# Bonus sums in a hybrid RWKV block: two 128x512 products become four float32 strips, and a transfer spreads the result

## The chip, the cores and the metric

The kernel runs on one core of one Trainium2 chip. The metric is the device time of one execution in microseconds; before the change it is 992.68 us, the median of three runs (991.85 to 993.29). A further execution was profiled. It took 991.71 us; its span, from the first to the last instruction, is 989.6 us, so 2.1 us lie around the span. In this text a place like "at 293.8" is a time in that span in microseconds.

## What is computed

One layer of a streaming encoder on 528 positions (16 learned meta tokens and 512 frames) of width 2048. One input projection with 8320 columns feeds two groups: an RWKV-7 time mixing with 16 heads of 64, and a short gated convolution with 1024 channels. Cut to what matters here:

```
P  = rmsnorm(h) @ w_in                     # 2048 x 8320
r, k, v, g_r = token-shifted columns of P  # 1024 wide each, 16 heads x 64
kk = (k * k_k) per head, divided by its norm
k  = k * (1 + (a - 1) * k_a)
y  = delta-rule recurrence of r, decay, k, v, kk, kk * a   # per head
yn = group norm of y per head
bonus = sum over the head of (r * k * r_k), times v
y_a = (yn + bonus) * silu(g_r)
y_b = B * conv3(C * h) * silu(g_c)
out = rmsnorm(h_res + concat(y_a, y_b) @ w_out)
```

The change concerns the line of the bonus. For every head and position there is one number, the sum of 64 products; it is multiplied with the 64 channels of v.

## The kernel before, in words

**Precision.** The large projections run as products of float32r parts. Every operand is split into a high part (a cast on ScalarE) and a low part (a subtraction on VectorE), and three of the four products are added up in PSUM. A tile of the input projection is 128 columns wide; its 2048 rows of contraction are done as four quarters of 512, and each quarter of weights has its own cast (L151) and its own subtraction (L152), `w<-wr` in the trace. TensorE takes the quarters one after another (L353 for the tiles with a token shift, L368 for the tiles B and gc).

**Order.** TensorE follows an order written out by hand. The tiles of the projection are a stream (`mains`); between its matmuls stands the rest of TensorE's work. `fill(ns)` takes so many estimated nanoseconds of stream matmuls. `later(ns, fn)` puts a transfer or an operation into the program when the stream has advanced by ns from now, and `until("v", i)` runs the stream until v of pair i exists. VectorE, ScalarE, GpSimd and the queue of SyncE (SP) are ordered by a scheduler from the order of the code and from priorities; on each of them an instruction that waits holds up all that stand behind it.

**Pairs.** The 16 heads are worked on as 8 pairs; a pair is a tile of 128 rows, 64 for each head. `prepare(i)` computes for pair i the decays, the operands of the recurrence (`ar`, `bk`), the Gram matrices `gt` (L755, L766), and the inverses of 16x16 blocks (`d`, `nd`, `y`, `prod`, `tt`: a chain of some thirty small VectorE operations, L855 to L888). The chain starts with `tt<-d,nd` (L862). Two pairs then go through `invert`.

**Norms of the keys.** The squared norms are sums over the 64 rows of a head. `key_norms` (L786) computes them as four matmuls in plain float32: 128 rows by 32 columns of a 0/1 matrix (`cs`), each with 144 positions and each in a column strip of its own of the array. The result lies in the first PSUM bank of the next stream tile, which is borrowed for this; `n2` (L781, `n` in the trace) takes it to SBUF, and two small stores (`sn<-n`) and a load (`nd<-sn`) bring it into the layout of the chain.

**Bonus.** After r, k and r_k have been multiplied in place into `r` (L735), `r` is split (L665 on ScalarE, L666 on VectorE). Two float32r matmuls with a 128x128 matrix `ones` (L820, L821) sum over the 64 rows of each head and at once spread the sum over 64 rows, into the bank `zb`. ScalarE copies `zb` back to `r` (L822), VectorE multiplies by v (L919), and the product is stored (`rbd<-r`, L920) until the output stage loads it.

**Convolution group.** A tile h is scaled in two halves by VectorE (`hh`, L404, with a small `ex`, L403, between them). GpSimd multiplies (`u`, L485), ScalarE takes the first tap (`cv`, L487), and VectorE adds the other two (L490). In the program these stand among the casts and subtractions of the weights. The second group of such tiles is called C1, h1, B1, gc1 here; it comes right behind pair 3.

Of the kernel before, what the change touches and what calls it, by code (L numbers as in the profile page):

```python
# [9 lines left out]
F32 = mybir.dt.float32  # L10
F32R = mybir.dt.float32r
I32 = mybir.dt.int32
AF = mybir.ActivationFunctionType
ALU = mybir.AluOpType
# [4 lines left out]
P = 128  # L19
DM = 2048  # L20
KT = DM // P
SEQ = 512
META = 16
L = SEQ + META
CH = 64
NCH = SEQ // CH + 1
LP = NCH * CH
# [5 lines left out]
C_ID, C_GM, C_BM, C_ON = 0, 128, 384, 512  # L33
# [11 lines left out]
    tr=3200, lev=3000, cp=4200, out=1500, begin=19500, p=2900, u=2900, s=4200, mid=1000, last=3700, mix=2600,  # L45
# [44 lines left out]
def hymba_kernel(ctx: ExitStack, tc: tile.TileContext, xt, xtok, front, w_in, w_out, pv, lup, cst, msk, gf, out):  # L90
    nc = tc.nc
    ctx.enter_context(tc.manual_schedule(engines={mybir.EngineType.PE}))
    cp = ctx.enter_context(tc.tile_pool(name="cp", bufs=1))
    dp = ctx.enter_context(tc.tile_pool(name="dp", bufs=2, space=DRAM))
# [3 lines left out]
    cs = cp.tile([P, C_N], F32, name="cs")  # L98
# [6 lines left out]
    rbd = [dp.tile([P, SEQ], F32, tag=f"rbd{j}", name=f"rbd{j}", bufs=1) for j in range(NPAIR)]  # L105
# [63 lines left out]
    xp = ph1.enter_context(tc.tile_pool(name="xp", bufs=1))  # L169
# [3 lines left out]
    rst = xp.tile([P, 4], F32, name="rst")  # L173
    rsx = cq.tile([P, 2 * META], F32, name="rsx")
    la = cq.tile([P, 2, L], F32R, name="la")
    ones = xp.tile([P, P], F32R, name="ones")
    omm = xp.tile([P, 33], F32, name="omm")
    hv = xp.tile([P, 6, 8], F32, name="hv")
    hl = cp.tile([P, 2, 8], F32, name="hl")
# [3 lines left out]
    pi = ph1.enter_context(tc.tile_pool(name="pi", bufs=1, space=PSUM))  # L183
# [5 lines left out]
    def tr(name, dt=F32):  # L189
        return cq.tile([P, LP], dt, tag="tr", name=name, bufs=5)  # L190
# [122 lines left out]
    with tc.issue_after(head):  # L313
        nc.vector.tensor_scalar(
            out=omm, in0=pvt[:, V_MU : V_MU + 33], scalar1=-1.0, scalar2=1.0, op0=ALU.mult, op1=ALU.add
        )
        for d, off in (
# [4 lines left out]
                out=d, in0=pvt[:, off : off + 8], scalar1=0.5, scalar2=None, op0=ALU.mult  # L322
            )
        nc.vector.tensor_scalar(
            out=hv[:, 4], in0=pvt[:, V_KA : V_KA + 8], scalar1=-0.5, scalar2=1.0, op0=ALU.mult, op1=ALU.add
        )

    nc.scalar.copy(ones, cs[:, C_BM : C_BM + P])
    FULL = ((0, 272), (272, L))
    TAIL = ((14, 272), (272, L))  # L330
    REAL = ((META, L),)
# [264 lines left out]
    def later(ns, fn):  # L596
        pending.append((clock[0] + ns, fn))
        pending.sort(key=lambda e: e[0])
# [60 lines left out]
        nc.vector.tensor_tensor(out=lo, in0=raw, in1=hi.bitcast(F32), op=ALU.subtract)  # L659
        return hi, lo  # L660

    def split(t, name, n):
        hi = tr(f"{name}_h", F32R)[:, 0:n]
        lo = tr(f"{name}_l", F32R)[:, 0:n]
        nc.scalar.copy(hi, t)  # L665
        nc.vector.tensor_tensor(out=lo, in0=t, in1=hi.bitcast(F32), op=ALU.subtract)  # L666
        return hi, lo

    heads = [(h, slice(64 * h, 64 * h + 64), slice(64 - 64 * h, 128 - 64 * h)) for h in range(2)]

    place = [(i % 2) * 4 + i // 2 for i in range(NPAIR)]
# [11 lines left out]
    def behind(dst, src):  # L683
        with tc.issue_after(state["dma"]):
            nc.sync.dma_start(dst, src)
# [8 lines left out]
    def prepare(i):  # L694
# [22 lines left out]
            out=bk[:, :, 0], in0=c3(k), scalar=hv[:, 2, i : i + 1], in1=c3(te), op0=ALU.mult, op1=ALU.mult  # L717
# [3 lines left out]
            out=ta, in0=ta, scalar1=hv[:, 3, i : i + 1], scalar2=hv[:, 4, i : i + 1], op0=ALU.mult, op1=ALU.add  # L721
        )
        nc.vector.scalar_tensor_tensor(
            out=ar[:, :, 0], in0=c3(k), scalar=col(V_KK, i), in1=e1[:, :, 0:CH], op0=ALU.mult, op1=ALU.mult
# [6 lines left out]
        r = got["r", i]  # L731
        nc.vector.tensor_tensor(
            out=ar[:, 1:NCH, 1], in0=c3(r), in1=e1[:, 1:NCH, 1 : CH + 1], op=ALU.mult
        )
        nc.vector.scalar_tensor_tensor(  # L735
            out=r, in0=r, scalar=hv[:, 5, i : i + 1], in1=ta[:, CH:LP], op0=ALU.mult, op1=ALU.mult
        )

        sq = tr(f"sq{i}")
        nc.scalar.activation(sq, k, AF.Square, scale=col(V_KK, i))  # L740
        rh, rl = split(r, f"rk{i}", SEQ)
        fill(FW["gram_b" if p else "gram"] + FW["meta"].get(i, 0))

        late = state["step"] > 48
# [16 lines left out]

        def gram_meta():
            z = early or next_banks()
            norms = key_norms(z[0][:, 96 : 96 + NS]) if late else None
            for h, hs, ho in heads:
                nc.tensor.matmul(  # L766
                    z[h][:, 0:META],
                    bk[hs, 0, h : h + 2, :].rearrange("p a s -> p (a s)"),
                    ar[hs, 0, 0, 0:META],
                    start=True, stop=True,  # L770
                )
            norms = norms if late else key_norms(z[0][:, 96 : 96 + NS])
            if p and "levels" in state:
                state["out"] = state.pop("levels").pop(0)(second_level(z))
            with ahead():
                for h in range(2):
                    nc.vector.tensor_tensor(
                        out=gt[:, h, 0, 0:META], in0=z[h][:, 0:META], in1=gmask[:, h, 0:META], op=ALU.mult
                    )
            with ahead():  # L780
                nc.scalar.copy(n2, norms)  # L781
            if "out" in state:
                state.pop("out")()
            state["banks"] = z

        def key_norms(z):  # L786
            for j in range(4):
                nc.tensor.matmul(
                    z[32 * j : 32 * j + 32], cs[:, C_BM + 48 : C_BM + 80], sq[:, j * NS : (j + 1) * NS],
                    start=True, stop=True, tile_position=(0, 32 * j),  # L790
                )
            return z
# [11 lines left out]

        NS = LP // 4
        n2 = tr(f"n2{i}")[:, 0:NS]
        if late:
            gram_meta()
        za = [pz.tile([P, 4, P], F32, tag="tz", name=f"g{i}_1_{h}") for h in range(2)]
# [6 lines left out]
        masked(zc, 5, 9)  # L816
        fill(FW["gram2"] - FW["meta"].get(i, 0))

        zb = pi.tile([P, SEQ], F32, tag="ser", name=f"zb{i}")
        nc.tensor.matmul(zb, ones[:, 0:P], rh, start=True, stop=False)  # L820
        nc.tensor.matmul(zb, ones[:, 0:P], rl, start=False, stop=True)  # L821
        nc.scalar.copy(r, zb)  # L822
        fill(FW["misc"])


# [4 lines left out]
        sg = dp.tile([SCR], F32, tag="sg", name=f"sg{i}")  # L830
        sn = dp.tile([2 * LP], F32, tag="sn", name=f"sn{i}")
        sx = scr_x[i % 2]

        def rows(t, h):
            return bass.AP(tensor=t.tensor, offset=t.offset + h * NCH * 4 * BLK, ap=[[CH, CH], [4 * BLK, NCH], [1, CH]])
# [3 lines left out]

        for h in range(2):  # L840
            behind(sn[h * LP : (h + 1) * LP].rearrange("(j s) -> j s", s=NS), n2[16 - 16 * h : P : 32])
        for h in range(2):
            behind(rows(sg, h), gt[64 * h : 64 * h + 64, h, :, 0:CH])
        NB = 8 * NCH
# [23 lines left out]
        for m in (2, 4, 8):  # L868
            for b in range(16 // (2 * m)):
# [4 lines left out]
                    out=pq,  # L874
                    in0=sub(d, o, o + m, [[16, m], [0, m], [1, m]]),
                    in1=sub(y, o + m, o + m, [[0, m], [1, m], [16, m]]),
                    op=ALU.mult,
                )
                nc.vector.tensor_reduce(
                    out=tq.rearrange("p (i j) -> p i j", i=m), in_=pq, op=ALU.add, axis=AX.X  # L880
                )
                nc.vector.tensor_tensor(
                    out=pq,
                    in0=sub(y, o, o, [[16, m], [0, m], [1, m]]),
                    in1=bass.AP(tensor=tq.tensor, offset=tq.offset, ap=[list(tq.ap[0]), [0, m], [1, m], [m, m]]),
                    op=ALU.mult,
# [19 lines left out]
        for h, hs, ho in heads:  # L906
            for b in range(2):
                for a in range(2):
                    later(9000 + 900 * (4 * h + 2 * b + a), lambda h=h, b=b, a=a: nc.sync.dma_start(
                        bass.AP(  # L910
                            tensor=bd.tensor,
                            offset=bd.offset + (h ^ a) * (NCH - 1) * CH * NPAIR * P + place[i] * P + 64 * h + 32 * b,
# [3 lines left out]
                    ))  # L916
        until("v", i)
        v = got["v", i]
        nc.vector.tensor_tensor(out=r, in0=r, in1=v[:, CH:LP], op=ALU.mult)  # L919
        later(12500, lambda: nc.sync.dma_start(rbd[i], r))  # L920
        fill(FW["v"])

        vs = cq.tile([P, NCH, CH], F32, tag="vs", name=f"vs{i}")
# [1 line left out]
        for b in range(4):  # L925
            for t in range(2):
                later(14000 + 1000 * (2 * b + t), lambda b=b, t=t: nc.sync.dma_start(
                    bass.AP(
                        tensor=vd.tensor,
# [736 lines left out]
```

## Time and profile before

| | before |
|---|---|
| median of three runs | 992.68 us |
| the profiled execution | 991.71 us |
| its span | 989.6 us |
| TensorE busy | 980.0 us, 99% |
| VectorE busy | 706.8 us, 71% |
| ScalarE busy | 390.6 us, 39% |
| GpSimd busy | 127.8 us, 13% |
| TensorE's share of the chain that ended last | 95% |

The matmuls overlap in the trace, so the duration of one is longer than the time it takes from its successor. What a matmul costs TensorE is read from the start of it to the start of the next. In rows of the timeline the columns are: start, duration of the merged instructions, engine, line, operation, output and inputs by their names, size of the tile of the array, moving operand, count, and in brackets the idle time before and what ended it.

### The profile page before, as it was taken

To read this page: it belongs to the slowest core of one execution; us is meant where nothing else is said; L and a number is where in the kernel's file an instruction comes from. 1 tells how busy PE (TensorE), PEld (TensorE's weight loads), DVE (VectorE), ACT (ScalarE), POOL (GpSimd) and SP (SyncE) were. 2 spreads that over 40 slices of the span, in tenths; PEclk is the share of its full clock that TensorE was granted. 3 is DMA by queue.
4 is the path that set the end of the run, shared out by engine and by line. 5 is a ranking of instruction groups with operands and counts; after the bars stand their busy time and mean duration, and the time that the engine had idled before them with its cause. 6 is when DMAs were issued, how large, how long until landed. Compare 5 with 4: busy or idle time off the path is not lost.

```text
span 989.6 us, 23395 instructions
## 1 busy us (share of the span) xinstructions
PE 980.0 (99%) x9511; PEld 907.5 (92%) x9511; DVE 706.8 (71%) x1413; ACT 390.6 (39%) x731; POOL 127.8 (13%) x242
## 2 busy tenths in 40 slices
PE   9999999999999999999999999999999999999996
PEld 9999999999998999998999998889889898788885
DVE  7777966578675779653778654365756697998896
ACT  7553432343322434322434323232323335446454
POOL 0110302112010111010111010011211102001001
PEclk9999999999999999999999999999999999999999
DMA  9526586246684375853275856999886697697554
GB/s 325 156 91 152 143 206 164 82 130 145 153 199 150 92 187 123 209 153 115 89 176 125 202 143 192 275 253 258 229 267 167 181 300 182 180 320 189 150 128 171
DMA packets 205532, 176.91 MB, mean 179 GB/s; under 512 B 138544, under 2 KB 168048, under 8 KB 205040
## 3 DMA queue, kind: packets, MB, share of 16 engines
q1 hardware_dynamic: 202832, 166.50, 60.2%
q0 software_dynamic: 2304, 8.39, 5.0%
q8 instruction: 75, 1.23, 0.5%
q10 hardware_dynamic: 288, 0.52, 0.1%
q14 instruction: 33, 0.27, 0.1%
HBM read 139.02 MB, written 36.35 MB: 177 GB/s over the span
## 4 chain that ended last, share of the span: by engine, by line
PE 95%; DVE 3%; ACT 1%; issue 1%; DMA 0%; DVEq 0%; POOL 0%; ACTq 0%
PE ps_v L353 9%; PE ps_h L353 9%; PE ps_C L353 9%; PE ps_g L353 9%; PE ps_B L368 9%; PE ps_gc L368 9%; PE ps_k L353 8%; PE ps_r L353 8%; PE M L1383 5%; PE P L1383 4%; PE Q L1383 2%; PE g L755 2%; PE ps_k L368 1%; PE ps_r L368 1%; PE ps_lora L368 1%; PE zy L1141 1%
## 5 line engine op out<-in xcount | busy, mean ns | idle before, releaser
L151 ACT CAST w<-wr 128x512 fp32r<-128x512 f32 x252 | 153.7, 619 | 285.1 <-PE ps_C L353 44.8
L152 DVE TENSOR_TENSOR w<-wr,w 128x512 fp32r<-128x512 f32 x252 | 174.8, 705 | 116.4 <-ACT w L151 115.5
L353 PE MATMUL ps_v<-xh,w 128*128 128x256 f32 (+2 forms) x512 | 84.0, 285 | 0.0
L368 PE MATMUL ps_B<-xh,w 128*128 128x512 f32 x256 | 83.4, 394 | 0.0
L353 PE MATMUL ps_h<-xh,w 128*128 128x256 f32 (+2 forms) x512 | 81.7, 281 | 0.0
L353 PE MATMUL ps_g<-xh,w 128*128 128x256 f32 (+2 forms) x512 | 81.4, 281 | 0.0
L368 PE MATMUL ps_gc<-xh,w 128*128 128x512 f32 x256 | 81.2, 392 | 0.0
L353 PE MATMUL ps_C<-xh,w 128*128 128x256 f32 (+2 forms) x512 | 80.8, 280 | 0.0
L353 PEld LDWEIGHTS ps_v<-xh,w 128*128 128x128 f32 x512 | 73.9, 188 | 0.3
L353 PE MATMUL ps_k<-xh,w 128*128 128x256 f32 (+1 forms) x448 | 73.4, 285 | 0.0
L353 PEld LDWEIGHTS ps_g<-xh,w 128*128 128x128 f32 x512 | 72.0, 189 | 0.6 <-issue 0.2
L353 PE MATMUL ps_r<-xh,w 128*128 128x256 f32 (+1 forms) x448 | 72.5, 280 | 0.0
L353 PEld LDWEIGHTS ps_h<-xh,w 128*128 128x128 f32 x512 | 72.1, 189 | 0.3
L353 PEld LDWEIGHTS ps_C<-xh,w 128*128 128x128 f32 x512 | 71.8, 189 | 0.2
L353 PEld LDWEIGHTS ps_k<-xh,w 128*128 128x128 f32 x448 | 64.7, 188 | 0.4
L353 PEld LDWEIGHTS ps_r<-xh,w 128*128 128x128 f32 x448 | 63.5, 189 | 0.4 <-issue 0.2
L353 PE MATMUL ps_h<-xl,w 128*128 128x256 f32 x256 | 57.3, 281 | 0.0
L368 PEld LDWEIGHTS ps_gc<-xh,w 128*128 128x128 f32 x256 | 47.8, 188 | 10.0
L368 PEld LDWEIGHTS ps_B<-xh,w 128*128 128x128 f32 x256 | 47.8, 188 | 9.7
L353 PE MATMUL ps_C<-xl,w 128*128 128x256 f32 x256 | 56.2, 280 | 0.0
L353 PE MATMUL ps_v<-xl,w 128*128 128x256 f32 x256 | 55.8, 278 | 0.0
L353 PE MATMUL ps_g<-xl,w 128*128 128x256 f32 x256 | 55.4, 278 | 0.0
(382 smaller groups left out, 2144.5 us busy)
## 6 DMA issues: line engine op xcount, KB each, us to landing
wr<-in_w_in_dram SPq DMA_DIRECT2D x126, 512.0 KB
ct<-opd SPq DMA_DIRECT2D x72, 192.0 KB
wo<-in_w_out_dram SPq DMA_DIRECT2D x24, 512.0 KB
x<-in_w_out_dram POOLq DMA_DIRECT2D x16, 512.0 KB, 5.6
opd<-ar SPq DMA_DIRECT2D x8, 576.0 KB
opd<-gt SPq DMA_DIRECT2D x16, 288.0 KB
bd<-bt SPq DMA_DIRECT2D x64, 64.0 KB
bw<-bd SPq DMA_DIRECT2D x16, 256.0 KB
```

Of the source, the lines that this page charges most:

```text
L151: nc.scalar.copy(hi, rq)
L152: low[q] = eng.tensor_tensor(out=lo, in0=rq, in1=hi.bitcast(F32), op=ALU.subtract).ins
L353: nc.tensor.matmul(ps[r][:, 0 : b - a], ww[:, k * P : (k + 1) * P], xx[:, kt, a:b], start=(kt == 0 and n == 0), stop=(kt == KT - 1 and n = ...
L368: nc.tensor.matmul(ps[r], ww[:, w], xx[:, kt, a:b], start=(kt == 0 and n == 0), stop=(kt == KT - 1 and n == 2))
L755: nc.tensor.matmul(z[h][:, c - c0], bk[hs, c, h : h + 2, :].rearrange("p a s -> p (a s)"), ar[hs, c].rearrange("p a s -> p (a s)"), start= ...
L1141: nc.tensor.matmul(zy[e][hs if e else ho, k], t[hs, o : o + CH], x, start=(n == 0), stop=(n == 2))
L1383: nc.tensor.matmul(bank[s], left(prod, jj, m, s), w, start=(jj == 0 and n == 0), stop=(jj == 7 and n == 2))
```

## The change

The split of `r`, the matrix `ones`, the bank `zb` and its copy go. The four float32 strips of `key_norms` become a function of their input (`head_sums`), which is called twice in a row: on the squared keys with 144 positions each, into the first borrowed bank, as before; and on `r` itself with 128 positions each, into the second borrowed bank. A copy of 128x128 on ScalarE (`nb`) stands behind that of the norms. Two stores of 4x128 numbers (`sb<-nb`) are put in 1000 ns later, a load of 128x512 that repeats each of the two rows over 64 partitions (`r<-sb`) 4500 ns later. The product with v is no longer done where v exists but 10500 ns after that place, and its store 15500 ns after it instead of 12500.

```
@@ prepare(i)
-        rh, rl = split(r, f"rk{i}", SEQ)
...
         def gram_meta():
             z = early or next_banks()
-            norms = key_norms(z[0][:, 96 : 96 + NS]) if late else None
+            if late:
+                norms, bonus = sums_of(z)
...
-            norms = norms if late else key_norms(z[0][:, 96 : 96 + NS])
+            if not late:
+                norms, bonus = sums_of(z)
...
             with ahead():
                 nc.scalar.copy(n2, norms)
+                nc.scalar.copy(nb, bonus)
...
-        def key_norms(z):
+        def sums_of(z):
+            return head_sums(z[0][:, 96 : 96 + NS], sq, NS), head_sums(z[1][:, 96 : 96 + P], r, P)
+
+        def head_sums(z, x, n):
             for j in range(4):
                 nc.tensor.matmul(
-                    z[32 * j : 32 * j + 32], cs[:, C_BM + 48 : C_BM + 80], sq[:, j * NS : (j + 1) * NS],
+                    z[32 * j : 32 * j + 32], cs[:, C_BM + 48 : C_BM + 80], x[:, j * n : (j + 1) * n],
                     start=True, stop=True, tile_position=(0, 32 * j),
                 )
             return z
...
-        zb = pi.tile([P, SEQ], F32, tag="ser", name=f"zb{i}")
-        nc.tensor.matmul(zb, ones[:, 0:P], rh, start=True, stop=False)
-        nc.tensor.matmul(zb, ones[:, 0:P], rl, start=False, stop=True)
-        nc.scalar.copy(r, zb)
...
+        for h in range(2):
+            later(1000, lambda h=h: nc.sync.dma_start(
+                sb[h * SEQ : (h + 1) * SEQ].rearrange("(j s) -> j s", s=P), nb[16 * h : P : 32]
+            ))
+        later(4500, lambda: nc.sync.dma_start(r, bass.AP(tensor=sb.tensor, offset=sb.offset, ap=[[SEQ, 2], [0, CH], [1, SEQ]])))
...
-        nc.vector.tensor_tensor(out=r, in0=r, in1=v[:, CH:LP], op=ALU.mult)
-        later(12500, lambda: nc.sync.dma_start(rbd[i], r))
+        later(10500, lambda: nc.vector.tensor_tensor(out=r, in0=r, in1=v[:, CH:LP], op=ALU.mult))
+        later(15500, lambda: nc.sync.dma_start(rbd[i], r))
```

The first place where the order of instructions changes is TensorE in each pair: the two products with `ones` stand between stream matmuls, at pair 1 at the end of a tile g. Before, TensorE at pair 1:

```order
L353 MATMUL ps_g_1_1663<-xl,w_1495 128x256 x4
L353 MATMUL ps_g_1_1663<-xh,w_1495 128x260 x4
L353 MATMUL ps_g_1_1663<-xh,w_1495 128x258 x3
L820 MATMUL zb_1808<-rk_h,ones 128x512
L821 MATMUL zb_1808<-rk_l,ones 128x512
L353 MATMUL ps_g_1_1663<-xh,w_1495 128x258
L353 MATMUL ps_C_0_1742<-xl,w_1555 128x256
```

After the change that place holds stream matmuls alone. The strips stand about 25 rows earlier, behind those of the norms; of the changed kernel, TensorE at pair 1 (`g_5` and the first two `ps_C` rows are the Gram matrices, `sq` the squared keys, `r` the products to be summed):

```order
L745 MATMUL g_5_0_1721<-ar_1355,bk_1356 128x128
L745 MATMUL g_5_1_1722<-ar_1355,bk_1356 128x128
L757 MATMUL ps_C_0_1739<-ar_1355,bk_1356 128x16
L757 MATMUL ps_C_1_1740<-ar_1355,bk_1356 128x16
L784 MATMUL ps_C_0_1739<-sq_1539,cs 32x144 x4
L784 MATMUL ps_C_1_1740<-r_1309,cs 32x128 x4
L351 MATMUL ps_g_1_1659<-xh,w_1370 128x258 x3
```

Two matmuls are gone from one place, and four strips stand at another, right behind strips of the same shape.

The second place is VectorE at the start of pair 3's chain, in the last tile before h1. `ex<-ps_C` can only run when TensorE has finished tile C1. Before:

```order
L861 COPY y_3669<-nd_3666 72x16
L152 TENSOR_TENSOR w_3752<-wr_3747,w_3752 128x512
L862 TENSOR_TENSOR tt_3674<-d_3665,nd_3666 72x8
L863 TENSOR_TENSOR y_3669<-tt_3674,nd_3666 72x8
L873 TENSOR_TENSOR prod_3673<-d_3665,y_3669 72x8
L948 STREAM_TRANSPOSE xn_4065<-xT_3080 128x512
L879 TENSOR_REDUCE tt_3674<-prod_3673 72x4
L882 TENSOR_TENSOR prod_3673<-y_3669,tt_3674 72x8
L152 TENSOR_TENSOR w_3781<-wr_3779,w_3781 128x512
L888 TENSOR_REDUCE y_3669<-prod_3673 72x2x2
L403 TENSOR_TENSOR ex<-ps_C_1_3513,rst 128x4
```

After, on the same engine and at the same place:

```order
L860 COPY y_3672<-nd_3669 72x16
L152 TENSOR_TENSOR w_3756<-wr_3751,w_3756 128x512
L401 TENSOR_TENSOR ex<-ps_C_1_3514,rst 128x4
L861 TENSOR_TENSOR tt_3677<-d_3668,nd_3669 72x8
L918 TENSOR_TENSOR r_3151<-r_3151,v_3325 128x512
L862 TENSOR_TENSOR y_3672<-tt_3677,nd_3669 72x8
L872 TENSOR_TENSOR prod_3676<-d_3668,y_3672 72x8
L947 STREAM_TRANSPOSE xn_4071<-xT_3081 128x512
L878 TENSOR_REDUCE tt_3677<-prod_3676 72x4
L881 TENSOR_TENSOR prod_3676<-y_3672,tt_3677 72x8
L887 TENSOR_REDUCE y_3672<-prod_3676 72x2x2
L152 TENSOR_TENSOR w_3786<-wr_3784,w_3786 128x512
```

The chain's first seven operations, the transpose `xn` among them, and one subtraction of weights stand behind the `ex` of tile C1 now, not ahead of it, and the product with v stands among them; before, that product stood some twenty rows earlier.

The third place is VectorE at the end of the same chain. Before:

```order
L873 TENSOR_TENSOR prod_3673<-d_3665,y_3669 72x512
L879 TENSOR_REDUCE tt_3674<-prod_3673 72x64
L882 TENSOR_TENSOR prod_3673<-y_3669,tt_3674 72x512
L888 TENSOR_REDUCE y_3669<-prod_3673 72x8x8
L404 TENSOR_TENSOR hh_4007<-ps_h_0_3884,rs 128x256
L403 TENSOR_TENSOR ex<-ps_h_1_3885,rst 128x4
L404 TENSOR_TENSOR hh_4007<-ps_h_1_3885,rs 128x256
L490 SCALAR_TENSOR_TENSOR cv_4014<-u_3870,pvt,cv_4014 128x512 x2
```

After:

```order
L872 TENSOR_TENSOR prod_3676<-d_3668,y_3672 72x512
L878 TENSOR_REDUCE tt_3677<-prod_3676 72x64
L402 TENSOR_TENSOR hh_4013<-ps_h_0_3889,rs 128x256
L881 TENSOR_TENSOR prod_3676<-y_3672,tt_3677 72x512
L401 TENSOR_TENSOR ex<-ps_h_1_3890,rst 128x4
L402 TENSOR_TENSOR hh_4013<-ps_h_1_3890,rs 128x256
L887 TENSOR_REDUCE y_3672<-prod_3676 72x8x8
L488 SCALAR_TENSOR_TENSOR cv_4020<-u_3875,pvt,cv_4020 128x512 x2
```

The two halves of `hh` have moved ahead of the chain's last reduction.

More of the change, by code (lines that the diff above doesn't have):

```diff
@@ L175, in hymba_kernel @@
     la = cq.tile([P, 2, L], F32R, name="la")
-    ones = xp.tile([P, P], F32R, name="ones")
     omm = xp.tile([P, 33], F32, name="omm")
@@ L326, in hymba_kernel @@
         )
-    nc.scalar.copy(ones, cs[:, C_BM : C_BM + P])
     FULL = ((0, 272), (272, L))
@@ L660, in lora_up @@
         return hi, lo
[L662 to L667, printed above, removed]
     heads = [(h, slice(64 * h, 64 * h + 64), slice(64 - 64 * h, 128 - 64 * h)) for h in range(2)]
@@ L806, in prepare @@
         n2 = tr(f"n2{i}")[:, 0:NS]
+        nb = tr(f"nb{i}")[:, 0:P]
         if late:
@@ L832, in prepare @@
         sx = scr_x[i % 2]
+        sb = dp.tile([2 * SEQ], F32, tag="sb", name=f"sb{i}")
         def rows(t, h):
```

## The prediction, as it was put on record

> **What bounds the kernel now.** I read the page's busy times and chain first, then the list of waits on TensorE.
>
> ```profile
> span 989.6 us, 23395 instructions
> PE 980.0 (99%) x9511; PEld 907.5 (92%) x9511; DVE 706.8 (71%) x1413; ACT 390.6 (39%) x731; POOL 127.8 (13%) x242
> PE 95%; DVE 3%; ACT 1%; issue 1%; DMA 0%; DVEq 0%; POOL 0%; ACTq 0%
> ```
>
> ```profile
> PE pwarm L202 <- DVE cold L199: 1.0, 1, 1.0
> PE M L1383 <- DVE o L1352: 0.3, 1, 0.3
> ```
>
> TensorE is busy for 99% of the span and carries 95% of the chain. In the whole run it waits twice, 1.3 us together, and neither wait lies where the change works. So a microsecond saved on another engine is worth nothing, one on TensorE is worth itself, and the change can lose only by making TensorE wait where it does not wait now. I therefore count TensorE's matmuls first and then look for the place where the other engines come close to it.
>
> **The change on TensorE.** The two products with `ones`, at pair 4, and the four strips of the key norms, at pair 1:
>
> ```profile
> 399.05 0.39 PE L820 MATMUL zb<-rk_h,ones 128*128 128x512 f32 x1
> 399.28 0.39 PE L821 MATMUL zb<-rk_l,ones 128*128 128x512 f32 x1
> 399.50 0.28 PE L353 MATMUL ps_g<-xl,w 128*128 128x256 f32 x1
> ...
> 122.62 0.45 PE L788 MATMUL ps_C<-sq,cs 128*32 128x144 f32 x8
> 122.76 0.31 PE L788 MATMUL ps_C<-sq,cs 128*32 128x144 f32 x4
> 123.00 0.39 PE L353 MATMUL ps_g<-xh,w 128*128 128x258 f32 x1
> ```
>
> Start to start, the two products cost 399.50 - 399.05 = 0.45 us. The strips of the norms cost 123.00 - 122.62 = 0.38 us: the first stretch lasts 0.14 us (122.62 to 122.76), and the last one 0.24 us with the way back to the stream in it. Eight new strips in the same form, right behind, should repeat the inner part alone: two stretches of 0.14 us, shortened from 144 to 128 positions, 2 x 0.14 x 128/144 = 0.25 us. The trace has no second set behind a first one, so I bound this: below by 0.12 us (one stretch, if the sets overlap), above by 0.38 us (a set of its own with all its ends). I take 0.25, because both new and old strips write disjoint strips of the array in the same way. The gain is 0.45 - 0.25 = 0.20 us in each of 8 pairs, 1.6 us in all; by the bounds 0.07 to 0.33 a pair, 0.6 to 2.6 us.
>
> [...]
>
> **What goes from and comes to the other engines.**
>
> ```profile
> L665 ACT CAST rk_h<-r x8: 620/621/624, 76.6 to 529.7; 128x512 fp32r<-128x512 f32 x8
> ...
> L822 ACT COPY r<-zb x8: 579/587/589, 89.0 to 546.8; 128x512 f32<-128x512 f32 x8
> ...
> L781 ACT COPY n<-ps_C x2: 278/278/279, 124.2 to 258.1; 128x144 f32<-128x144 f32 x2
> ...
> L666 DVE TENSOR_TENSOR rk_l<-r,rk_h x8: 677/690/694, 78.4 to 530.4; 128x512 fp32r<-128x512 f32 x8
> ...
> L919 DVE TENSOR_TENSOR r<-r,v x8: 685/692/694, 89.7 to 547.4; 128x512 f32<-128x512 f32 x8
> ...
> L685 SPq DMA_DIRECT2D sn<-n x16: 494/538/607, 85.8 to 544.9; - x16
> ```
>
> Per pair ScalarE loses a cast (0.62) and a copy (0.59) and gains a copy of about 0.28; VectorE loses a subtraction (0.69) and keeps its product (0.69); SyncE's queue gains two small stores of about 0.54 and the issue of one load. ScalarE is busy 39% of the span and VectorE 71%, so by themselves these are worth nothing. The second borrowed bank is free again when the new copy has read it, at pair 1 some 0.6 us behind 124.2, and the tile that owns it begins only here:
>
> ```profile
> 129.52 0.28 PE L353 MATMUL ps_C<-xl,w 128*128 128x256 f32 x1
> ```
>
> The loads of weights behind the new issues start a microsecond or two later. What hides that is in the page's row of the casts:
>
> ```profile
> L151 ACT CAST w<-wr 128x512 fp32r<-128x512 f32 x252 | 153.7, 619 | 285.1 <-PE ps_C L353 44.8
> ```
>
> The idle time ahead of them is ended by TensorE, which frees their buffers, and not by a landing: the loads are early. Were that cover gone, each microsecond would be one of TensorE's.
>
> **The place where it bites: tile B1, behind pair 3.** The order shows pair 3's chain entering VectorE behind `ex` of tile C1 instead of ahead of it. VectorE of before:
>
> ```profile
> 273.19 0.15 DVE L862 TENSOR_TENSOR tt<-d,nd 72x8 f32<-72x8 f32 x1
> ...
> 274.44 0.16 DVE L882 TENSOR_TENSOR prod<-y,tt 72x8 f32<-72x8 f32 x1
> 275.32 0.69 DVE L152 TENSOR_TENSOR w<-wr,w 128x512 fp32r<-128x512 f32 x1 [0.71 <-ACT w L151]
> 275.93 0.15 DVE L888 TENSOR_REDUCE y<-prod 72x4 f32<-72x8 f32 x1
> 277.42 0.16 DVE L403 TENSOR_TENSOR ex<-ps_C,rst 128x4 f32<-128x4 f32 x1 [1.34 <-PE ps_C L353]
> ...
> 287.20 0.68 DVE L888 TENSOR_REDUCE y<-prod 72x64 f32<-72x512 f32 x1
> 287.80 0.41 DVE L404 TENSOR_TENSOR hh<-ps_h,rs 128x256 f32<-128x256 f32 x1
> 288.65 0.16 DVE L403 TENSOR_TENSOR ex<-ps_h,rst 128x4 f32<-128x4 f32 x1 [0.44 <-PE ps_h L353]
> 288.73 0.41 DVE L404 TENSOR_TENSOR hh<-ps_h,rs 128x256 f32<-128x256 f32 x1
> ...
> 292.85 2.49 DVE L152 TENSOR_TENSOR w<-wr,w 128x512 fp32r<-128x512 f32 x4
> ```
>
> Today VectorE does the chain's start in time that it would otherwise spend waiting (1.34 us) for TensorE to end C1. After that `ex` it runs almost without a gap: from 277.42 to the end of the first `hh`, 287.80 + 0.41 = 288.21, are 10.79 us. With the change the following stands behind the `ex` as well: the chain's start with the transpose, 273.19 to 274.44 + 0.16, 1.41 us; its first reduction, 0.15; one subtraction, 275.93 - 275.32 = 0.61; and the product with v, of the same size, 0.61. That is 2.78 us. The last reduction, 0.60 (287.20 to 287.80), goes behind `hh`. So 10.79 + 2.78 - 0.60 = 12.97 us. By then TensorE has gained 4 x 0.20 = 0.80 us, so `ex` starts at 276.62, the first `hh` ends at 289.59, and with `ex` (0.08) and the second `hh` (0.41) VectorE is there at 290.08. Before it was 288.73 + 0.41 = 289.14: 0.94 us later.
>
> Behind `hh` stands a tail that the change leaves alone, on GpSimd, ScalarE and TensorE:
>
> ```profile
> 289.29 1.30 POOL L485 TENSOR_TENSOR u<-u,hh 128x514 f32<-128x514 f32 x1
> ```
>
> ```profile
> 290.63 0.73 ACT L487 ACTIVATE cv<-u,pvt 128x512 f32<-128x512 f32 x1 [10.42 <-POOL u L485]
> 291.26 2.17 ACT L151 CAST w<-wr 128x512 fp32r<-128x512 f32 x4
> ```
>
> ```profile
> 293.62 0.62 PE L368 MATMUL ps_B<-xh,w 128*128 128x512 f32 x2
> 294.08 0.39 PE L368 MATMUL ps_B<-xl,w 128*128 128x512 f32 x1
> 294.30 0.62 PE L368 MATMUL ps_B<-xh,w 128*128 128x512 f32 x2
> ```
>
> GpSimd's `u` waits for `hh`, ScalarE's `cv` for `u`, and queued behind `cv` are four casts of weights; VectorE's four subtractions stand behind its two `cv`. The first of them starts at 292.85 and is done 0.69 us later, 293.54. It is the low part for the fourth quarter of B1. That quarter begins with the second of the two matmuls at 293.62 (293.85), goes on with `xl` at 294.08, and takes the low part with the first of the two at 294.30. So the weights come 0.76 us ahead of TensorE, the closest place I found; TensorE has none of this to wait for today. Afterwards they come at 293.54 + 0.94 = 294.48, while TensorE, 0.80 us early, wants them at 293.50: a wait of 0.98 us that is not there now. The lead cancels, as the chain starts with an `ex` that TensorE releases; the wait is 2.78 - 0.60 less the idle 0.44 us before the second `ex` and the slack of 0.76. It could be nothing if VectorE's operations follow each other faster by 1 us over these 13 us, or about 1.8 us if something else is 0.8 us late with them.
>
> **Sum**, against the profiled execution of 991.71 us, 0.97 us under the median of 992.68: -1.6 + 0.98 = -0.6 us, 991.1, or on the scale of the median **992.1 us**.
>
> **The load that spreads the sums.** Ahead of pair 3's product stand on SyncE's queue and on VectorE:
>
> ```profile
> 266.81 0.53 SPq L685 DMA_DIRECT2D nd<-sn  x1
> ...
> 268.90 0.32 SPq L685 DMA_DIRECT2D d<-sg  x1
> ```
>
> ```profile
> 269.02 0.17 DVE L855 TENSOR_SCALAR nd<-nd 72x16 f32<-72x16 f32 x1 [1.38 <-DMA nd<-sn]
> ```
>
> ```profile
> x<-in_w_out_dram POOLq DMA_DIRECT2D x16, 512.0 KB, 5.6
> ```
>
> The two stores come behind `nd<-sn`, and 2 x 0.54 us fit ahead of 268.90; the load comes behind `d<-sg`, at about 269.3. It also waits for the stores to land, with a load of weights queued behind it; small transfers land soon, `nd<-sn` 2.2 us after its issue. The product stands second behind `ex`, near 276.9, so the load has some 7.6 us. It is unlike every transfer of the trace (256 KB written from 4 KB), so I bound it by the small 2.2 us and the 5.6 us of a load twice its size. Both ends fit, and I cost it at nothing. Beyond 7.6 us each microsecond would stop VectorE's in-order queue in front of the chain, and go into the wait at B1 in full.
>
> **Rivals.**
> 1. *The gain without the wait.* If VectorE is 1 us quicker through the chain or the quarter is needed later, -1.6 stays: 991.1 us. For it: the wait is a small difference of long sums. Against: those rows are nearly gapless.
> 2. *The strips overlap more than I allow*, 0.12 us: -2.6 us, 990.1 without the wait. For it: the profile shows the first stretch of four strips take 0.14 us. Against: two stretches are seen in every set.
> 3. *Slower: the load lands late at pair 3.* It decides from a landing 7.6 us after the issue. At 11 us, twice the 5.6 us of the row, the wait at B1 is 0.98 + 3.4 = 4.4 us: +2.8, 995.5. For it: 128 rows read two short stretches of memory again and again, beside weights and `opd` transfers. Against: it moves half the bytes of the 5.6 us load.
> [...]
>
> **How the numbers follow.** The forecast has a chance of 0.56, rival 1 0.19, rival 2 0.09, rival 3 0.14, rival 4 0.02. The forecast's own range is 991.4 to 993.6: the wait at 0.3 to 1.8 with strips at 0.25 to 0.34. A difference of about 0.2%, 2 us, is what a measurement of this kernel can tell from no change; both the forecast and rival 1 lie inside it. So same 0.75, faster 0.09, slower 0.16. For 8 in 10 the range goes from just above rival 2 to within rival 3: 990.4 to 994.8.
>
> **What would show it.** Right: TensorE's list of waits gains one entry at `ps_B` near 293.5, about 1 us, on a subtraction of weights; the strips cost 0.25 us more a pair; the second `hh` of h1 ends near 290.1; TensorE waits nowhere else. Wrong: no such wait (rival 1); VectorE idle in front of the product with v on the load, several microseconds (rival 3); a strips' set of 0.9 us (rival 4); or a wait in another pair, whose chains I followed less closely than pair 3's.

## The result, and the profile after

The changed kernel takes 1004.94 us (median of 4 runs, 1003.34 to 1007.24), against 992.26 us for the kernel before in the same comparison: a ratio of 1.0134, 95% interval 1.0122 to 1.0146. It is 12.7 us slower, where 992.1 with a range to 994.8 was predicted. The page and the waits of TensorE after the change:

```profile
span 1001.6 us, 23499 instructions
...
PE 983.3 (98%) x9559; PEld 908.8 (91%) x9559; DVE 702.9 (70%) x1405; ACT 381.7 (38%) x722; POOL 124.6 (12%) x242
...
PE 70%; DVE 12%; DMA 12%; issue 2%; ACT 2%; SPq 2%; POOL 1%; DVEq 0%; ACTq 0%
```

```profile
PE ps_B L366 <- ACT w L151: 2.3, 1, 2.3
PE ta L633 <- ACT tz L638: 2.0, 2, 1.2
PE t L962 <- DVE xn L947: 1.5, 3, 0.8
PE ps_gc L366 <- ACT w L151: 1.2, 1, 1.2
...
PE ps_B L366 <- DVE w L152: 0.9, 1, 0.9
PE ta L633 <- ACT tz L640: 0.4, 1, 0.4
...
PE ps_gc L366 <- DVE w L152: 0.3, 1, 0.3
PE g L745 <- DVE bk L718: 0.2, 1, 0.2
```

VectorE and ScalarE have less to do, as the diff says. But transfers, 0% of the chain before, carry 12% of it now, and eight kinds of wait on TensorE are new, 8.8 us together. Among the longest single pieces of the chain that ended last are transfers, in order of time (start, length, what):

```profile
90.46 9.02 DMA r<-sb
...
139.30 9.34 DMA r<-sb
...
221.30 7.62 DMA d<-sg
...
274.49 10.02 DMA wr<-in_w_in_dram
```

`r<-sb` is the new load. `d<-sg` and the load of weights at 274.49 are old ones that come behind it. VectorE at pair 3:

```profile
279.93 0.16 DVE L401 TENSOR_TENSOR ex<-ps_C,rst 128x4 f32<-128x4 f32 x1
280.00 0.15 DVE L861 TENSOR_TENSOR tt<-d,nd 72x8 f32<-72x8 f32 x1
283.23 0.69 DVE L918 TENSOR_TENSOR r<-r,v 128x512 f32<-128x512 f32 x1 [3.08 <-DMA r<-sb]
...
295.69 0.40 DVE L402 TENSOR_TENSOR hh<-ps_h,rs 128x256 f32<-128x256 f32 x1
```

The product stands second behind `ex`, as the order said, and waits there 3.08 us for the load; the second `hh` ends at 296.09, not at 290.1. TensorE then waits at B1 and goes on at half speed. Of the stretches below, the columns are the stretch, its length, the busy time of the five engines, the granted clock, the DMA share and GB/s:

```profile
300.00:302.50 2.50, 2.01 (x5) 1.63 (x6) 2.24 (x4) 0.33 (x1) 1.32 (x4) 0.50 0.17 40
302.50:305.00 2.50, 2.50 (x8) 1.91 (x7) 0.00 (x0) 0.00 (x0) 0.00 (x0) 0.50 0.73 154
```

Before the change the clock stays at 1.00 through this whole tile. From the starts of TensorE's matmuls in the two traces, the lag behind the kernel before is 2.5 us when B1's second quarter starts (291.13 and 293.64) and 9.0 us at the first of gc1 (300.57 and 309.60). So B1 alone costs 6.5 us: 3.2 us of waits, and most of the rest is the clock, 0.50 for 6.8 us: the matmuls in it start 0.43 us apart, where 0.23 us is usual. The other places: 2.0 at gc0, 0.7, 1.6 and 1.0 at `ta` of pairs 3, 5 and 7, and five smaller ones, 2.6 together. Against these 14.4 us stands the gain of the strips, about 2 us.

### The profile page after: what moved, and what is told of

Read it like the earlier page. It is cut to its first block, busy times and chain, and to the rows that moved or that the text cites. A ratio compares the mean times of both kernels' runs of the same rounds, so it can differ in the third digit from the quotient of the medians.

```text
span 1001.6 us, 23499 instructions
## 1 busy us (share of the span) xinstructions
PE 983.3 (98%) x9559; PEld 908.8 (91%) x9559; DVE 702.9 (70%) x1405; ACT 381.7 (38%) x722; POOL 124.6 (12%) x242
## 4 chain that ended last, share of the span: by engine, by line
PE 70%; DVE 12%; DMA 12%; issue 2%; ACT 2%; SPq 2%; POOL 1%; DVEq 0%; ACTq 0%
PE ps_B L366 9%; PE ps_gc L366 8%; PE ps_v L351 6%; PE M L1382 5%; PE ps_g L351 5%; PE ps_C L351 5%; PE ps_h L351 5%; PE ps_r L351 5%; PE ps_k L351 5%; PE P L1382 4%; DMA d<-sg 2%; DMA r<-sb 2%; DMA sx<-y 2%; PE Q L1382 2%; DVE w L152 2%
## 5 line engine op out<-in xcount | busy, mean ns | idle before, releaser
L151 ACT CAST w<-wr 128x512 fp32r<-128x512 f32 x252 | 152.3, 619 | 295.0 <-DMA wr<-in_w_in_dram 59.7
L366 PE MATMUL ps_B<-xh,w 128*128 128x512 f32 x256 | 85.9, 404 | 3.2 <-ACT w L151 2.3
L366 PEld LDWEIGHTS ps_gc<-xh,w 128*128 128x128 f32 x256 | 47.8, 188 | 12.2 <-ACT w L151 1.6
```

Of the source, the lines that this page charges most:

```text
L151: nc.scalar.copy(hi, rq)
L366: nc.tensor.matmul(ps[r], ww[:, w], xx[:, kt, a:b], start=(kt == 0 and n == 0), stop=(kt == KT - 1 and n == 2))
```

## Experiments

All were run beside the kernel before; a ratio is to that kernel, with its 95% interval.

### Is it the strips and the order, or the transfer?

e1_no_transfer: the stores and the load go, the product takes `r` unsummed.

```
-        later(1000, ... sb <- nb)      # both stores
-        later(4500, ... r <- sb)       # the load
```

> The strips and the copy nb stay; the two stores and the load that spreads the sums are left out, so the product with v uses r unsummed (the bonus is left out in that sense). Theory A (VectorE's in-order queue waits on the load): all waits that the change brought go, and what is left is the strips, -0.24 us in each of 8 pairs: 1.9 us under before, about 990.4, TensorE's list of waits as before. Theory B (the strips or the other order of VectorE cost the time): stays at 1000 or more.

Measured: 989.09 us, ratio 0.9974 (0.9964 to 0.9984), and no new wait over 0.5 us on TensorE. So the strips and the copy cost TensorE nothing that shows; they gain 2.6 us, between 1.6 and 3.6. Of the moved chain this run tells nothing: without the load the scheduler puts the start of pair 3's chain ahead of `ex` of C1 again.

e2_load_unwaited: stores and load stay, but nobody reads what is loaded.

```
-        later(4500, ... dma_start(r, ...sb...))
+        later(4500, ... dma_start(rl, ...sb...))   # rl: a tile of its own
```

> Stores and load stay with their traffic, but the load goes into a tile of its own that nobody reads; the product uses r unsummed. The chain of pair 3 stands behind ex of C1 here, without the product in it. Theory A (the wait): no wait on the load; by the prediction's sum without the product (0.61) the wait at B1 is about 0.4 us, so 990.4 to 991.0. Theory C (the traffic itself delays weights and blocks of the inverses): ScalarE still waits about 60 us for weights, TensorE waits several times, 996 or more.

Measured: 1003.32 us, ratio 1.0120 (1.0100 to 1.0139). Theory A, that the loss is VectorE's wait on the product, falls: without that wait the kernel is as slow. TensorE waits 2.5 us at B1 (2.3 in the changed kernel), and VectorE, which doesn't wait for the load now, waits for others (12.1 us for `d<-sg`, 2.5 in the changed kernel):

```profile
DVE tt L862 <- DMA d<-sg: 12.1, 4, 4.2
```

```profile
277.86 0.15 DVE L862 TENSOR_TENSOR tt<-d,nd 72x8 f32<-72x8 f32 x1
...
282.62 1.29 DVE L152 TENSOR_TENSOR w<-wr,w 128x512 fp32r<-128x512 f32 x2 [2.76 <-ACT w L151]
```

At pair 3 the chain has begun and is stopped 2.76 us by a subtraction whose weights have not landed: the cast ahead of it waits 4.90 us for `wr`. Here it is the weights that are late in VectorE's row, in the changed kernel the product (3.08 us). That the load slows the other transfers is what the next two runs test.

e6_before_plus_load and e7_before_plus_rows put one unread load per pair into the kernel before, and edit nothing else. The scheduler then moves a few rows of VectorE, in e6, e7, e12 and e13 alike: these four have the same order on VectorE, ScalarE, GpSimd and SyncE.

```
+        rl = cq.tile([P, SEQ], F32, ...)
+        later(4500, ... dma_start(rl, two rows, each for 64 partitions))   # e6
+        later(4500, ... dma_start(rl, 128 different rows))                 # e7
```

> The kernel before with one load more per pair at the place where the change has its own: two adjacent rows of 2 KB from the output weights, each repeated over 64 partitions, into a tile that nobody reads. Nothing is left out. Theory D: the load alone holds up the weights and blocks behind it, 996 to 1005, with waits at B1 and at L633 of the odd pairs as after the change. Rival (the loss needs the new order on VectorE or the wait of the product): 991 to 993.

> As e6_before_plus_load, but the load takes 128 different rows. Theory D: 991 to 993, no new waits over 0.5 us. Rival (any load of 256 KB at this place costs it): as e6_before_plus_load.

Measured: e6 1004.02 us, ratio 1.0126 (1.0108 to 1.0144); e7 991.84 us, ratio 0.9996 (0.9988 to 1.0005). The load alone costs 12 us on a kernel that has neither strips nor the new order; a load of the same bytes from 128 rows costs nothing. In e6's chain a store of four rows of 144 numbers takes 6.84 us behind the load of pair 4; one takes 1.57 in the changed kernel where no such load is ahead of it (at 86.20):

```profile
355.64 6.84 DMA sn<-n
...
505.94 6.42 DMA sn<-n
```

### Why is this load slow?

e3_load_other_rows, e4_eight_copies and e5_two_copies change the rows that the load of the changed kernel reads.

```
+  e3: load w_out[0, 0][:, 0:512], 128 rows; the sums are not loaded
+  e4: stores write each row of sums 8 times; load ap=[[SEQ, 16], [0, 8], [1, SEQ]]
+  e5: stores write each row of sums 2 times; load ap=[[SEQ, 4], [0, 32], [1, SEQ]]
```

> The load takes 128 different rows of 2 KB from the output weights in place of the two rows of sums repeated over 64 partitions; all else stays, the output uses those weights as sums. Theory D (the repeated rows make the load slow): it lands in 5 to 6 us after its issue, not 7.8 to 9.4, and VectorE waits for it 0 to 1.5 us in place of 3 to 4: 991 to 995. Theory E (the load waits behind other transfers): it lands after 7.5 to 9.5 us as before, and the time stays at 1001 to 1007.

> The stores write each row of sums eight times, and the load reads 16 different rows, each for 8 partitions; nothing is left out. The scheduler puts the product some 28 rows later at pair 3 and 12 to 26 later at pairs 0 and 1. Theory D (repeated rows): landing in 5 to 6.5 us. Theory E (behind other transfers): 7.5 to 9.5 us. Theory A: with the product that late it waits under 0.5 us at the odd pairs either way, B1 gets its weights within 1 us, and the time falls to 990.5 to 993; theory B: no change from 1005.

> As the changed kernel, but the stores write each row of sums twice and the load reads 4 rows, each for 32 partitions. The order on VectorE is the same, row for row, as in the changed kernel. Theory D, graded (the landing grows with the partitions that read one row: 64 took 7.8 to 9.4 us, 8 at most 3.9): 32 take about 6 us, the product waits under 1 us, the time falls to 991 to 996; and if the load is no longer late at pair 3, what is left at B1 tests the prediction's 0.98 us. Theory D, in a step (any row read by many is slow): landing and time as in the changed kernel, 1001 to 1007.

Measured: e3 990.25 us, 0.9986 (0.9977 to 0.9995); e4 992.01 us, 1.0005 (0.9996 to 1.0014); e5 991.21 us, 0.9991 (0.9982 to 1.0000). From issue to the product that waits for it, the load takes 7.75 to 9.4 us in the changed kernel, 6.2 to 7.2 in e5 and 5.4 to 5.8 in e3; in e4 the product starts 3.9 us behind the issue at pair 2 and waits for nothing. With VectorE's order the same row for row, e5 is 13.7 us faster than the change. Reads of the same rows looked like the cause (theory D), and the next run was to show that more of them cost more.

e12_before_plus_one_row is e6 with one row for all 128 partitions:

```
+        later(4500, ... ap=[[0, P], [1, SEQ]])
```

> As e6_before_plus_load, but one row of 2 KB for all 128 partitions in place of two rows for 64 each. If reads of one row are served one after another, the load lasts longer than the 8 to 9 us seen for 64, and the kernel takes 1010 or more; if it is a fixed penalty for repeated reads, 1002 to 1007 as e6_before_plus_load.

Measured: 991.97 us, ratio 1.0000 (0.9992 to 1.0009), which neither of the two expectations allowed. One row read 128 times costs nothing, so theory D falls too. What sets the slow sources apart is their shape: two groups of 64. Two runs separate shape from repetition. e13_two_halves_rows has the shape and reads each row once; e14_two_loads reads each row 64 times without the shape.

```
+  e13, on the kernel before: ap=[[P * 1024 + SEQ, 2], [1024, CH], [1, SEQ]]
+  e14, on the changed kernel, for each h: dma_start(r[64 * h : 64 * h + 64], ap=[[0, CH], [1, SEQ]])
```

> As e7_before_plus_rows (the kernel before, one unread load of 128 different rows more per pair), but the rows come as two groups of 64 with a gap between the groups, so that the source has an outermost dimension of two, as in the change; no row is read twice. [...] Theory D (repeated rows): 991 to 993 as e7_before_plus_rows.

> As the changed kernel, but the load is written as two, one per head: 64 partitions each, all from the same row of 2 KB. Each row is still read 64 times; the outermost dimension is 64 in place of two. [...] Theory D: landing 7.5 us or later, 1000 or more.

Measured: e13 1005.49 us, ratio 1.0137 (1.0115 to 1.0159); e14 991.49 us, ratio 0.9992 (0.9983 to 1.0001). Theory D had 991 to 993 for e13 and 1000 or more for e14 and is wrong on both sides: the shape brings the loss without a row read twice, and 64 reads of each row without the shape bring none (what e14 still waits is 0.9 us at B1 and 0.5 us at gc0). The stretches in which the load runs differ as well; first e13 and e6 with an outermost dimension of 2, then e4 with 16:

```profile
354.60:359.70 5.10, 5.10 (x45) 5.10 (x44) 1.54 (x4) 0.62 (x1) 0.15 (x1) 1.00 0.19 66
```

```profile
356.70:361.70 5.00, 5.00 (x44) 5.00 (x43) 1.58 (x4) 0.62 (x1) 0.15 (x1) 1.00 0.18 66
```

```profile
219.30:220.60 1.30, 1.30 (x13) 1.30 (x12) 0.24 (x1) 0.57 (x1) 0.00 (x0) 1.00 1.05 258
```

The last two columns are the mean busy share of the 16 DMA engines and the rate. With 2 outermost, 256 KB go for 5 us at 66 GB/s and a share of 0.18; with 16 they go in 1.3 us at 258 GB/s and a share of 1.05. The trace's single packets say the same. In e6 at pair 4 the load's 128 packets of 2 KB run two at a time, 84 ns each, from 356.67 to 361.82; in the changed kernel it is 1.9 to 2.1 on average at pairs 0, 2, 4, 5, 6 and 7. In e5, with 4 outermost, 3.5 to 3.7 run at once on average at pairs 0, 2, 4 and 6; in e4, with 16, 10 to 12 at pairs 2, 4 and 6. They also show a transfer beside the load that waits: of the eight packets of the store `sn<-n` above, four start at 356.58 to 356.84 and the other four only at 361.80 to 361.85, when the load's last packet is ending. Why these four start so late was not shown: the trace does not tell the engine of a packet.

### Does another queue help?

e8_before_plus_load_act issues e6's load from ScalarE's queue; e11_before_plus_load_act does so behind the copy of the norms of its pair.

```
-        later(4500, ... nc.sync.dma_start(rl, ...))
+        later(4500, ... nc.scalar.dma_start(rl, ...))      # e8; e11 also: issue_after(copy n2)
```

> As e6_before_plus_load, but the load is issued from ScalarE's queue in place of SyncE's. Theory H (transfers of SyncE's queue wait behind it in order): with a queue of its own it holds up nobody, 991 to 993. Theory I (it slows the memory or the DMA engines that all queues share): 996 or more, as e6_before_plus_load.

> As e6_before_plus_load, but issued from ScalarE's queue, held behind the copy of the norms of its pair, some 5 us earlier than from SyncE's. Theory H (what is queued behind it on SyncE waits in order): 991 to 994, with weights and blocks as in before. Theory I (it slows the memory or the DMA engines that all queues share): 997 or more.

Measured: e8 1033.37 us, ratio 1.0413 (1.0399 to 1.0428), which tells nothing of the question: nothing held its loads back, the scheduler put them at the start of the kernel, and TensorE waits 11.5 and 10.1 us there. e11, with the loads in place: 999.35 us, ratio 1.0078 (1.0066 to 1.0090). This speaks for theory I: issued from ScalarE's queue the load still costs 7.7 us by the ratio. That it is less than e6's 12 may come from its issue, 0.5 to 16 us earlier in the span than in e6, or from VectorE's order, which is that of the kernel before row for row; neither was tried apart.

### The same load at a later place

e9_later_64 and e10_later_32 move stores, load and product behind the chain's start.

```
+  e9:  stores later(8000), load later(14000), product later(20000), rows as in the change
+  e10: the same places, each row of sums stored twice and read by 32 partitions
```

> As the changed kernel, but the two stores are put in 7000 ns later and the load 9500 ns later, and the product with v falls behind the chain of its pair; the load still repeats each row over 64 partitions. At pair 3 the chain starts ahead of ex of C1 again. Theory J (the load costs by what stands right behind it: blocks, norms and weights for the start of the chain): most of the loss goes, 990 to 994. Theory K (a load with rows repeated that often costs wherever it stands): 997 or more, with TensorE waiting at other places.

> As e9_later_64, with the same order on VectorE, but the rows stored twice and each read by 32 partitions. The strips' 1.9 us is kept and the wait of 0.9 us at B1 that e5_two_copies had goes: 989.5 to 991. If J is right, e9_later_64 is within 2 us of it; if K is right, e9_later_64 is 6 us or more above it.

Measured: e9 1001.53 us, ratio 1.0093 (1.0075 to 1.0111); e10 997.31 us, ratio 1.0053 (1.0041 to 1.0065). e9 lies where theory K put it, e10 missed its 989.5 to 991, and the 4.2 us between them lie between the 2 us of J and the 6 us of K. The waits at B1 are gone, but a new one of 4.9 us in e9 and 4.0 us in e10 stands at `t<-xn` of pair 1. SyncE of e10 there:

```profile
165.82 0.34 SPq L920 DMA_DIRECT2D rbd<-r  x1
166.26 0.38 SPq L159 DMA_DIRECT2D wr<-in_w_in_dram  x1
166.73 0.63 SPq L894 DMA_DIRECT2D xT<-sx  x1
```

The store of the product, which now exists only at 165.8, stands ahead of `xT<-sx`, which before went out at 161.56, and goes out at 166.73 now; `sx<-y`, which it needs, is 2.3 us later as well (155.99 and 158.26). So the place of the product has a price of its own in SyncE's queue; how much of e9's further 4.2 us is the load, the pair of runs does not tell exactly.

### What is left at B1, and a version that gains

With 4 rows outermost, e5 still waits 0.9 us at B1, the place and almost the size that the prediction gave (0.98):

```profile
PE ps_B L366 <- DVE w L152: 0.9, 1, 0.9
```

```profile
275.58 0.16 DVE L401 TENSOR_TENSOR ex<-ps_C,rst 128x4 f32<-128x4 f32 x1 [1.08 <-PE ps_C L351]
275.66 0.16 DVE L862 TENSOR_TENSOR tt<-d,nd 72x8 f32<-72x8 f32 x1
276.49 0.69 DVE L919 TENSOR_TENSOR r<-r,v 128x512 f32<-128x512 f32 x1 [0.68 <-DMA r<-sb]
...
288.89 0.40 DVE L402 TENSOR_TENSOR hh<-ps_h,rs 128x256 f32<-128x256 f32 x1
```

From `ex` to the end of the second `hh` are 13.71 us, 0.68 of them the wait on the load; without it 13.03, where the prediction had added up 13.46 (276.62 to 290.08). The sum was 0.4 us too long, and the load's wait, which it didn't have, made up for it. By the starts of the matmuls TensorE loses about 1.2 us here, of which the chain alone would then leave some 0.55, an estimate (1.2 less 0.68). Three runs take this place apart.

```
+  e15: as e5, and at pair 3 the stores at 2500 in place of 1000
+  e16: copies 2 at pairs 0 and 1, else 4; at pair 3 stores at 8000, load at 14000, product at 20000
+  e17: copies 2 at pairs 0 and 1, else 8; at pair 3 load at 14000, product at 20000
```

> As e5_two_copies, but at pair 3 alone the two stores are put in 2500 ns in place of 1000 ns after their place; the scheduler then leaves the first rows of pair 3's chain ahead of ex of C1 and puts the product with v some 19 rows later. Everything else stands as in e5_two_copies. If the prediction's account of B1 is right, the wait of 0.9 us there falls under 0.3 us, and the time goes from 991.2 to about 990.3; if the wait at B1 came from elsewhere, it stays.

> Sums and strips as in the change. Pairs 0 and 1 store each row of sums twice (source of 4 rows), the others four times (8 rows), and at pair 3 the stores come 7000 ns and the load 9500 ns later, so that the product with v stands behind the chain, both cv and the first two subtractions of weights. On VectorE four rows of pair 3's chain stand ahead of ex of C1, and one subtraction more than before lies inside it. By the prediction's account of B1 (slack 0.76 us, plus the 0.44 us it idles before the second ex, against 0.6 to 1.4 us added) the wait there is 0 to 0.3 us: 990 to 991, the first version clearly faster than before. If B1 keeps 0.7 us or more, that account is not the whole of it.

> As e16_copies_pair3_late_4, but eight copies from pair 2 on (a source of 16 rows) and at pair 3 only the load later; the whole start of the chain stands ahead of ex of C1, as before the change, with three subtractions of weights more inside. Load in under 4 us at the even pairs. 989.8 to 991.5, wait at B1 0 to 0.5 us.

Measured: e15 991.96 us, ratio 0.9994 (0.9985 to 1.0002); e16 989.28 us, ratio 0.9976 (0.9966 to 0.9985); e17 989.65 us, ratio 0.9981 (0.9972 to 0.9990). e15's wait fell only to 0.7, not under 0.3: the product was still in the chain there and waited 0.56 us for its load, so e15 does not decide. With the product behind the chain and the chain's start ahead of `ex`, TensorE's list of e16 is that of the kernel before:

```profile
PE pwarm L201 <- DVE cold L198: 1.0, 1, 1.0
PE M L1385 <- DVE o L1354: 0.3, 1, 0.3
```

e16 leaves nothing out, is 2.4 us faster than the kernel before by its ratio (1.5 to 3.4), and so keeps what e1 gained without a transfer.

## Why the prediction was wrong

**What bounds the kernel** was right: the lag of TensorE behind the kernel before grows where it waits or runs at half clock, at B1 from 2.5 to 9.0 us.

**The strips** were right, a little low. At pair 1 of the changed kernel:

```profile
122.36 0.45 PE L784 MATMUL ps_C<-sq,cs 128*32 128x144 f32 x8
122.63 0.40 PE L784 MATMUL ps_C<-r,cs 128*32 128x128 f32 x8
122.96 0.63 PE L351 MATMUL ps_g<-xh,w 128*128 128x258 f32 x3
```

Both sets take 0.60 us together, 0.22 more than the one of before; 0.25 was forecast. The removed products give back 0.47 a pair by the shift of the stream between the traces, against 0.45. So the gain is 0.25 a pair, 2.0 us, where 1.6 was forecast. Rival 4's 0.9 us for a set of strips, which has a chance of 0.02 in the forecast, is shown by no run: the new set takes 0.33 us with the way back to the stream. The "eight new strips" of the prediction are four strips, each of which the trace counts as two matmuls (x8 in the rows above).

**The wait at B1 behind the moved chain** was right in place and mechanism: e5 shows it at 0.9, and e16, which moves both the product and the chain's start, has none. Its size was 0.4 us too long in the chain's sum, as worked out above; that e5's 0.9 stands so near to 0.98 is luck, as 0.68 us of it come from the load. The quarter that waits is the third of B1, not the fourth: of its 48 matmuls 24 start at 293.85 or later. The sum does not depend on that.

**The step that failed is the load, "so I bound it by the small 2.2 us and the 5.6 us of a load twice its size. Both ends fit, and I cost it at nothing."** From its issue to the product that waits for it, it takes 7.75 to 9.4 us. The step reasoned from bytes. The transfer that served as the upper bound has 128 rows outermost, this one has two groups of 64, and e13 (1005.49 us) and e14 (991.49 us) show that this shape, not the bytes and not the repeated rows, decides. The prediction saw that the load "is unlike every transfer of the trace" and still took that row as an end; none of the rows it read has that shape, so the bound held nothing.

**Rival 3, the late load,** named the right transfer with a chance of 0.14, but for a reason that e12 and e14 rule out, rows read again and again; so it was right in part by luck. It put the decision 7.6 us after the issue: at pair 3 the product starts 9.35 us behind the issue (273.88 to 283.23) and waits 3.08 us, so it was 6.3. Its price of 2.8 us was low by 10. It counted one wait at one pair. But transfers behind the load are late as well, at pair 2 `d<-sg` with 7.62 us and at pair 3 a load of weights with 10.02 us, and by e2 (1003.32 us) the wait of the product isn't even needed. The cover that the prediction leaned on is gone in the page's row of the casts, where TensorE ended the idle time before:

```profile
L151 ACT CAST w<-wr 128x512 fp32r<-128x512 f32 x252 | 152.3, 619 | 295.0 <-DMA wr<-in_w_in_dram 59.7
```

The loads of weights end it now, 59.7 us of it (e3 has 47.8 without a loss, so most of that is harmless). And the price left out that a wait on TensorE can cost more than itself: at B1 3.2 us of waits became 6.5 with the clock.

**The range** took the far end from this rival at one pair; TensorE's new waits lie at gc0, at B1 and at `ta` of pairs 3, 5 and 7.

## What to carry to other kernels

Read the outermost dimension of a transfer's pattern before its bytes: at the place of the change a load with 2 outermost cost 12 us or more (ratios of 1.0126 in e6 and 1.0137 in e13), with 4, 16, 64 and 128 (e5, e4, e14, e12) the ratios are 0.9991 to 1.0005. So a load that repeats two rows over 64 partitions each should be written as two loads, or from copies. A transfer that nobody waits for can still cost 1% through what it delays (1.0120 in e2, 1.0126 in e6); putting it alone into the old kernel (e6) shows this in one run. When no row of the trace has the shape of a new transfer, leave the upper bound open and give the rival built on it a larger chance and the price of every pair.

## What the runs showed of the hardware that was not expected

In three runs the granted clock of TensorE fell to 0.50 after waits of 1.31 to 2.48 us, for 3.4 or 6.8 us. After the change it falls at 299.49, behind a wait of 2.30 us that ended at 298.82 and just ahead of the next one of 0.93 us, and stays for 6.8 us. In e2 it falls at 298.04, behind a wait of 2.48 us and inside one of 0.93 us, for 3.4 us; in e6 at 258.46, behind a single wait of 1.31 us (256.19 to 257.50), for 3.4 us. Yet the wait of 1.77 us at 377 in e6 leaves the clock at 1.00, so the length of a wait alone does not decide.

The places of the falls say more. In the changed kernel and in e6 they lie whole steps of 3.413 us apart: in e6 99 steps from 258.46 to the next fall at 596.38, after the change 204 steps from 299.49 to the fall behind the last matmuls at 995.81. The stretches below are such steps to within 0.05 us, the first two lines of the changed kernel, the others of e6; the second and the fifth follow on a fall:

```profile
296.08:299.49 3.41, 1.11 (x4) 0.32 (x3) 1.76 (x4) 1.95 (x4) 1.29 (x2) 1.00 0.74 136
299.49:302.90 3.41, 2.48 (x7) 1.93 (x7) 2.75 (x5) 0.84 (x2) 1.32 (x4) 0.50 0.29 60
234.56:237.97 3.41, 1.81 (x16) 1.62 (x15) 3.31 (x11) 1.59 (x3) 1.26 (x2) 1.00 1.06 210
255.04:258.45 3.41, 2.10 (x60) 1.75 (x60) 3.41 (x8) 0.73 (x2) 0.44 (x2) 1.00 0.47 66
258.50:261.90 3.40, 3.40 (x66) 3.33 (x53) 3.20 (x6) 0.80 (x2) 0.00 (x0) 0.50 1.00 302
374.51:377.92 3.41, 2.50 (x22) 2.29 (x20) 2.81 (x14) 0.46 (x1) 1.09 (x2) 1.00 0.95 211
377.92:381.33 3.41, 2.56 (x22) 2.56 (x22) 3.00 (x7) 2.20 (x6) 1.56 (x1) 1.00 0.91 169
```

The wait of 2.30 us lies in one step, in which TensorE is busy for 1.11 of 3.41 us; the wait at 377 is shared out over two steps with 2.50 and 2.56 us. That the place of a wait on these steps is what counts is an estimate from these two; no run shows it. Busy time does not decide alone either: the step from 234.56 has 1.81 us and is followed by full clock, the one from 255.04 has 2.10 us, most of it small matmuls, and is followed by half. What else counts stays open.
